# mLSTM values by direction with alternating head halves, queries split in the projections, output weights loaded over items 8 to 13

## The chip, the cores and the metric

The kernel runs on one core of a Trainium2 chip. The metric is device time in microseconds of one execution. In the rows of the profile PE is the matrix engine (TensorE), PEld its weight loads, DVE the vector engine, ACT the scalar engine, POOL GpSimd and SP the engine that issues the DMAs.

## The reference

One layer of a hybrid backbone in float32: 1024 latent tokens of width 1024, with 256 context tokens as a prefix. What the layer computes, cut to what matters:

```python
px = modulate(rms_norm(x, g_pre_mix), sh_m, sc_m) @ w_in        # pc: the same for ctx
aqx, akx, avx, mqx, mkx, mvx, mox, mgx = split(px)
att_x = window_attention(rope(aqx), rope(akx), avx, kc_att, vc_att, attn_sink)
    # 8 query heads of 64 on 2 key heads; one softmax over keys within 128,
    # all 256 context keys and a sink
h = mlstm_bidir(...)     # 4 heads, keys of 64, values of 128, forward plus backward scan:
    # num = (q k' * w_intra) v + w_inter * C q ; den = the same sums with v = 1
    # h = num / max(|den|, exp(-m))
ml_x = rms_norm(h) * g_mlstm_out * sigmoid(mox)
x = x + gt_m * rms_norm(concat(att_x, ml_x) @ w_out) * g_post_mix
x = x + gt_f * rms_norm(swiglu(modulate(rms_norm(x), ...))) * g_post_ffn
```

## The kernel before

Large products run as three passes: each operand is split into a high part in a rounded float32 format (`fp32r` in the rows) and the low rest, and `mm3` sums high*high, high*low and low*high in PSUM. `split` (L56) does it with an ACT cast (L58) and a DVE subtraction (L59). Matmuls on plain float32 operands, as in the mLSTM values, appear as two instructions each in the profile.

The stages follow each other: adaLN vectors and normalised tokens; the projections; attention with mLSTM; the output projection with the second norm; the feed-forward layer (from about 590 us to the end). The change touches the second, the third and the seam to the fourth.

**Projections** (about 140 to 306 us). Thirteen tiles of 128 output features (`TILES`: mLSTM keys and queries, attention keys and queries, output gates) are computed by `tproj` over 8 slices of the contraction, for 1024 tokens in two PSUM banks and, for three tiles, 256 context columns in a third. Four banks are in rotation. `conv` or `rope` empties them. An attention query tile (`aq0` to `aq3`) is rotated into buffer `s0` and stored to `aq_d` in DRAM by two DMAs (L619). Between tiles, `state_step` advances the mLSTM states of both directions: PE transposes keys, DVE weights them, PE multiplies with the values, DVE adds. DVE also accumulates the remaining adaLN rows (L492).

**Attention with mLSTM** (about 306 to 497 us) runs over 16 items: block n of 128 tokens times key head g. `Soft(i).scores(h)` multiplies a query head with up to 384 window keys and 256 context keys (L778, L779) and DVE masks and reduces (L780); `norm` takes exponentials on ACT (L789) and normalises on POOL (L794). `Values(i)` transposes the probabilities (`tr`, L808), splits them, and multiplies by the values (`mm`, L818, L819). Queries come from DRAM as one tile `qd` (`q_load`, L564) and are split by POOL (`q_split`, L570, L571). Scores are computed two items ahead.

Items 0 to 7 also do one block of mLSTM each: `ml_scores` of the next block (L693, eight half-height instructions that alternate the two 64-row head halves), `ml_values` four times (two directions times two head halves), `ml_norm`, and `ml_out` of the block before. One `ml_values` call takes one bank: for each of two head pairs a matmul of the query rows with the state (64 rows, L707) and one of the weights with V (128 rows, L708); then DVE forms the denominator (L711 to L713), and ACT (forward, L717) or DVE (backward, L719) scales the two heads out of the bank. `state()` tiles, mLSTM queries and weights live in the same 16 slots `R(k)` that the output weights take later.

PSUM in this stage: three banks `pt` for transposes, mLSTM values and `ml_out`, one bank `po`, and two double banks `s` for scores. `PLAN_ML` and `PLAN` give the order in which the steps of an item are written down. The order on each engine is made from it by a planner that plays the program through with costs of its own and lets ready instructions pass. From item 14 on, and in all later stages, the order is written by hand (`manual_schedule`): there items 14 and 15 are interleaved with the output projection of block 0, `omm(0, 1, ..)` for the mLSTM half and, at the end, `omm(0, 0, ..)` for the attention half, into `ops_[0]`.

The eight output weight tiles (`wout_load`) are read in the order 7 to 0 in items 9 to 13: DMA, an ACT cast (L749) and a POOL subtraction (L750); the last one goes in two halves through the buffers of `qd`, with ACT and DVE (L58, L59).

Of the kernel before, what the change touches and what calls it, by code (L numbers as in the profile page):

```python
# [16 lines left out]
P = 128  # L17
# [16 lines left out]
PLAN_ML = "T0 q A0 A1 A2 A3 T1 T2 T3 M0 M1 T4 V0 N0 M2 V1 M3 M4 O z V2 w V3 s N1 x"  # L34
PLAN = "T0 q A0 A1 A2 A3 T1 T2 T3 N0 M0 T4 M1 M2 N1 M3 M4 O z l"


def body(tc, x, ctx, vecs, bcv, bada, gqm, gqf, wada, ws1, ws2, wt, wout, wfi, wfo,
# [377 lines left out]
    aq_d = tc.dram_tile([8, 64, S], F32, name="aq_d")  # L416
# [13 lines left out]
    def tproj(j, with_ctx):  # L430
        wh, wl = tws.pop(j)
        ps = [pa.tile([P, 512], F32, name=f"t{j}_{i}", tag="mm", bufs=4) for i in range(3 if with_ctx else 2)]
        for kt in range(KT):
# [3 lines left out]
            if with_ctx:  # L437
                mov.append((ch[b][:, k, :], cl[b][:, k, :]))
            outs = [ps[0], ps[1]] + ([ps[2][:, :L]] if with_ctx else [])
            for o, m in zip(outs, mov):  # L440
                pe.matmul(o, wh[:, kt], m[0], start=f, stop=False)  # L441
                pe.matmul(o, wh[:, kt], m[1], start=False, stop=False)  # L442
            for o, m in zip(outs, mov):
                pe.matmul(o, wl[:, kt], m[0], start=False, stop=l)  # L444
        return ps
# [111 lines left out]
    qds, qhl, prs, wo = {}, {}, {}, {}  # L557
# [8 lines left out]
    def q_split(i):  # L566
        qd = qds.pop(i)
        qh = qq.tile([P, 4, P], F32R, name="qh", tag="qh", bufs=2)
        ql = qq.tile([P, 4, P], F32R, name="ql", tag="ql", bufs=2)
        pool.tensor_scalar(qh, qd, 1.0, 1.0, MUL, MUL)  # L570
        pool.tensor_tensor(ql, qd, qh.bitcast(F32), SUB)  # L571
        qhl[i] = qh, ql
# [16 lines left out]
    for j, name in enumerate(TILES):  # L589
# [38 lines left out]
        if name == "aq3":  # L628
# [3 lines left out]
            for i in range(2):  # L632
                q_load(i)
                q_split(i)
# [65 lines left out]
    def ml_values(n, d, hb):  # L700
# [3 lines left out]
        r = slice(hb * 64, hb * 64 + 64)  # L704
        pv = bank().rearrange("p a b -> p (a b)")[:, 0:258].rearrange("p (j v) -> p j v", j=2)
        for j in range(2):
            pe.matmul(pv[:, j, :], qp_[r, d, j, :], cs[r, j, :], start=True, stop=False)  # L707
            pe.matmul(pv[:, j, :], wt_[:, d, 2 * j + hb, :], V[:, n, 2 * j + hb, :], start=False, stop=True)  # L708
        dn = qa.tile([P, 2], F32, name="dn", tag="dn", bufs=8)
        den = pv[:, :, 128]  # L710
        dve.tensor_tensor(dn, den, emcol[:, r0 + hb:r0 + 4:2], MAX)  # L711
        dve.scalar_tensor_tensor(dn, den, -1.0, dn, MUL, MAX)
        dve.reciprocal(dn, dn)  # L713
        for j in range(2):
            t = hs[:, 2 * j + hb]
            if d == 0:
                act.activation(t, pv[:, j, 0:128], AF.Copy, scale=dn[:, j:j + 1])  # L717
            else:
                dve.scalar_tensor_tensor(t, pv[:, j, 0:128], dn[:, j:j + 1], t, MUL, ADD)  # L719
# [18 lines left out]
    def wout_load(j):  # L738
        h, l = R(2 * j, f"woh{j}", (D,), F32R), R(2 * j + 1, f"wol{j}", (D,), F32R)
        if j == 0:  # L740
            for i in range(2):
                sl = slice(i * 512, (i + 1) * 512)
                load_split(h[:, sl], l[:, sl], wout[j][:, sl],
                           qq.tile([P, 4, P], F32, name="wor0", tag="qd", bufs=2).rearrange("p a b -> p (a b)"))
            wo[j] = h, l
            return
        raw = R(2 * j - 1, f"wor{j}", (D,))
# [83 lines left out]
    for i in range(2):  # L831
# [5 lines left out]
        if i == 0:  # L837
            q_load(2)
            ml_scores(0)

    for i in range(NIT):
# [6 lines left out]
        for k in (PLAN_ML if i < NT else PLAN).split():  # L848
# [862 lines left out]
```

## Time and profile before

| | us |
|---|---|
| median of 3 runs (lowest, highest) | 1239.06 (1238.37, 1239.9) |
| the profiled execution, its own time | 1238.05 |
| its span | 1236.3 |
| projections of 13 tiles | about 140 to 306 |
| items 0 to 7 (with mLSTM) | about 310 to 437 |
| items 8 to 13 | about 437 to 482 |
| items 14 and 15, block 0 of the output projection | about 482 to 502 |

The granted clock of PE is full in all these stretches. Rows of grouped instructions give line, engine, operation, output and inputs, shapes, count, then busy microseconds, mean nanoseconds of one, and the idle time of the engine ahead of them with what ended it. Rows of a timeline give start and length in microseconds; a bracket holds the idle time before and its releaser. Rows of waits give the total, the count and the longest. Matmuls are pipelined: the distance between starts tells more than a row's length.

### The profile page before, as it was taken

To read this page: it belongs to the slowest core of one execution; us is meant where nothing else is said; L and a number is where in the kernel's file an instruction comes from. 1 tells how busy PE (TensorE), PEld (TensorE's weight loads), DVE (VectorE), ACT (ScalarE), POOL (GpSimd) and SP (SyncE) were. 2 spreads that over 40 slices of the span, in tenths; PEclk is the share of its full clock that TensorE was granted. 3 is DMA by queue.
4 is the path that set the end of the run, shared out by engine and by line. 5 is a ranking of instruction groups with operands and counts; after the bars stand their busy time and mean duration, and the time that the engine had idled before them with its cause. 6 is when DMAs were issued, how large, how long until landed. Compare 5 with 4: busy or idle time off the path is not lost.

```text
span 1236.3 us, 16232 instructions
## 1 busy us (share of the span) xinstructions
PE 1193.3 (97%) x5859; PEld 971.0 (79%) x5859; DVE 798.9 (65%) x1375; ACT 579.9 (47%) x1111; POOL 205.1 (17%) x245
## 2 busy tenths in 40 slices
PE   7889999999999998999899999999999999999996
PEld 1789878877777786888678888888888888888885
DVE  3882277862877787355767677767777746554566
ACT  4654533111666796677633333333333325434542
POOL 0752401244644475000000000000000000000000
PEclk9899999999999999999999999999999999999999
DMA  9432855656433320522024465675644647665853
GB/s 339 157 114 73 302 161 153 190 144 194 130 86 86 113 76 10 204 80 74 17 90 137 174 226 191 214 245 190 220 154 161 202 155 257 206 216 191 306 170 119
DMA packets 90953, 201.78 MB, mean 163 GB/s; under 512 B 9077, under 2 KB 29941, under 8 KB 89465
## 3 DMA queue, kind: packets, MB, share of 16 engines
q1 hardware_dynamic: 90872, 200.74, 48.8%
q8 instruction: 46, 0.75, 0.3%
q14 instruction: 35, 0.28, 0.1%
HBM read 149.32 MB, written 50.73 MB: 162 GB/s over the span
## 4 chain that ended last, share of the span: by engine, by line
PE 65%; DVE 4%; ACT 3%; POOL 1%; DMA 1%; issue 1%; DVEq 0%; ACTq 0%
PE xv L72 7%; PE xv L71 7%; PE xv L70 7%; PE pt L72 5%; PE pt L71 5%; PE pt L70 5%; PE pt L708 2%; PE pt L707 2%; PE pt L808 2%; PE fx L70 1%; PE op L72 1%; PE op L70 1%; PE op L71 1%; PE fx L72 1%; PE fx L71 1%; PE s L778 1%
## 5 line engine op out<-in xcount | busy, mean ns | idle before, releaser
L59 DVE TENSOR_TENSOR fo<-fr,fo 128x1024 fp32r<-128x1024 f32 x77 | 92.7, 1222 | 71.2 <-ACT fo L58 60.8
L58 ACT CAST fo<-fr 128x1024 fp32r<-128x1024 f32 x77 | 79.7, 1051 | 73.9 <-PE pt L72 36.5
L441 PE MATMUL t<-hh,th 128*128 128x512 f32 x208 | 82.6, 397 | 1.7 <-ACT cr L458 1.7
L442 PE MATMUL t<-hl,th 128*128 128x512 f32 x208 | 82.2, 395 | 0.0
L58 ACT CAST wS<-wr 128x512 fp32r<-128x512 f32 x88 | 54.1, 622 | 56.3 <-PE pt L72 37.4
L59 DVE TENSOR_TENSOR wS<-wr,wS 128x512 fp32r<-128x512 f32 x88 | 60.4, 689 | 19.9 <-ACT wS L58 19.9
L70 PE MATMUL xv<-tT,wS 128*128 128x512 f32 x168 | 66.9, 398 | 4.9 <-ACT tT L1083 2.3
L444 PE MATMUL t<-hh,tl 128*128 128x512 f32 x208 | 68.3, 393 | 0.0
L72 PE MATMUL xv<-tT,wS 128*128 128x512 f32 x168 | 66.2, 394 | 0.3 <-DVE wS L59 0.3
L71 PE MATMUL xv<-tT,wS 128*128 128x512 f32 x168 | 66.3, 395 | 0.0
L492 DVE SCALAR_TENSOR_TENSOR acc<-wb,csil,acc 128x1024 f32<-128x1024 f32 x24 | 34.4, 1432 | 40.1 <-DMA wb<-in_wada 40.0
L441 PEld LDWEIGHTS t<-hh,th 128*128 128x128 f32 x208 | 39.1, 188 | 10.4 <-ACT cr L458 2.1
L944 DVE TENSOR_TENSOR wr<-wr 128x512 f32<-128x512 f32 x66 | 45.5, 690 | 1.5
L1195 ACT ACTIVATE es<-es 128x512 f32<-128x512 f32 x22 | 13.9, 632 | 67.8 <-DVE es L947 67.8
L442 PEld LDWEIGHTS t<-hl,th 128*128 128x128 f32 x208 | 39.1, 188 | 8.1 <-issue 1.2
L444 PEld LDWEIGHTS t<-hh,tl 128*128 128x128 f32 x208 | 38.3, 188 | 7.9 <-issue 1.0
L70 PE MATMUL op<-woh,mh 128*128 128x512 f32 x112 | 44.3, 395 | 0.0
L72 PE MATMUL op<-woh,ml 128*128 128x512 f32 x112 | 43.8, 391 | 0.0
L71 PE MATMUL op<-wol,mh 128*128 128x512 f32 x112 | 43.7, 390 | 0.0
L72 PE MATMUL pt<-fo 128*128 128x512 f32 x110 | 42.8, 389 | 0.0
L71 PE MATMUL pt<-fo 128*128 128x512 f32 x110 | 42.8, 389 | 0.0
L70 PE MATMUL pt<-fo 128*128 128x512 f32 x110 | 42.8, 389 | 0.0
(982 smaller groups left out, 3491.0 us busy)
## 6 DMA issues: line engine op xcount, KB each, us to landing
wr<-in_wfi SPq DMA_DIRECT2D x44, 512.0 KB, 4.7
wb<-in_wada SPq DMA_DIRECT2D x24, 512.0 KB, 4.3
s_d<-a SPq DMA_DIRECT2D x22, 512.0 KB, 6.6
bt<-in_wfo SPq DMA_DIRECT2D x44, 256.0 KB, 3.6
tb_d<-bt SPq DMA_DIRECT2D x11, 1024.0 KB, 3.9
fr<-s_d SPq DMA_DIRECT2D x44, 256.0 KB, 4.2
fr<-tb_d SPq DMA_DIRECT2D x44, 256.0 KB, 4.5
fr<-a_d SPq DMA_DIRECT2D x33, 256.0 KB, 4.5
```

Source lines behind the costliest of these rows:

```text
L58: act.copy(hi, raw)
L59: dve.tensor_tensor(lo, raw, hi.bitcast(F32), SUB)
L70: pe.matmul(ps, a[0], b[0], start=first, stop=False, **kw)
L71: pe.matmul(ps, a[0], b[1], start=False, stop=False, **kw)
L72: pe.matmul(ps, a[1], b[0], start=False, stop=last, **kw)
L441: pe.matmul(o, wh[:, kt], m[0], start=f, stop=False)
L442: pe.matmul(o, wh[:, kt], m[1], start=False, stop=False)
L444: pe.matmul(o, wl[:, kt], m[0], start=False, stop=l)
L492: dve.scalar_tensor_tensor(a, t, csil[:, kt, 0:1], a, MUL, ADD)
L707: pe.matmul(pv[:, j, :], qp_[r, d, j, :], cs[r, j, :], start=True, stop=False)
L708: pe.matmul(pv[:, j, :], wt_[:, d, 2 * j + hb, :], V[:, n, 2 * j + hb, :], start=False, stop=True)
L944: dve.tensor_tensor(out, a, b, SUB)
```

## The change

`ml_values` takes a whole direction and two banks. It first does the four 64-row matmuls, alternating the head halves and with them the two banks, then the four 128-row ones; the reciprocal is taken once a direction. The four steps V0 to V3 of an item become V0 and V1.

The attention queries are split where they are projected (ACT and DVE); high and low part go to two DRAM tensors, and `q_load` fetches both. The step `q` is gone.

`tproj` does the context columns after the token columns.

The output weights are read in the order 0 to 7 in items 8 to 13, all with ACT and POOL, the raw tile in the slot of the next tile's high part. With them, the four attention-half steps of block 0's output projection (P0 to P3) move from the end of the hand-written part into item 13 (`PLAN13`).

```diff
-PLAN_ML = "T0 q A0 A1 A2 A3 T1 T2 T3 M0 M1 T4 V0 N0 M2 V1 M3 M4 O z V2 w V3 s N1 x"
-PLAN = "T0 q A0 A1 A2 A3 T1 T2 T3 N0 M0 T4 M1 M2 N1 M3 M4 O z l"
+PLAN_ML = "T0 A0 A1 A2 A3 T1 T2 T3 M0 M1 T4 V0 N0 M2 M3 M4 O z V1 w s N1 x"
+PLAN = "T0 A0 A1 A2 A3 T1 T2 T3 N0 M0 T4 M1 M2 N1 M3 M4 O z l"
+PLAN13 = "T0 A0 A1 A2 A3 m T1 T2 P0 T3 N0 M0 T4 M1 P1 M2 N1 M3 P2 M4 O P3 l"
+WLOADS = {8: (0, 1), 9: (2,), 10: (3,), 11: (4,), 12: (5, 6), 13: (7,)}
...
-    aq_d = tc.dram_tile([8, 64, S], F32, name="aq_d")
+    aq_d = [tc.dram_tile([8, 64, S], F32, name=f"aq_d{p}") for p in "hl"]
...
-            if with_ctx:
-                mov.append((ch[b][:, k, :], cl[b][:, k, :]))
...
+        for kt in range(KT if with_ctx else 0):
+            b, k = kt // 4, kt % 4
+            mm3(ps[2][:, :L], (wh[:, kt], wl[:, kt]), (ch[b][:, k, :], cl[b][:, k, :]), kt == 0, kt == KT - 1)
...
-        qd = qds[i] = qq.tile([P, 4, P], F32, name="qd", tag="qd", bufs=2)
-        for d in range(2):
-            dma(qd[64 * d:64 * d + 64], aq_d[4 * g:4 * g + 4, :, n * P:(n + 1) * P].rearrange("h d t -> d h t"))
...
-        pool.tensor_scalar(qh, qd, 1.0, 1.0, MUL, MUL)
-        pool.tensor_tensor(ql, qd, qh.bitcast(F32), SUB)
+        qhl[i] = [qq.tile([P, 4, P], F32R, name=f"q{p}", tag=f"q{p}", bufs=3) for p in "hl"]
+        for t, src in zip(qhl[i], aq_d):
+            for d in range(2):
+                dma(t[64 * d:64 * d + 64].bitcast(F32), src[4 * g:4 * g + 4, :, n * P:(n + 1) * P].rearrange("h d t -> d h t"))
...
             rope(ps, t, 0.125)
-            for g in range(2):
-                dma(aq_d[4 * g + i], t[64 * g:64 * g + 64])
+            qp2 = R(3, f"aqh{i}", (S,), F32R), t.bitcast(F32R)
+            split(*qp2, t)
+            for d, o in zip(aq_d, qp2):
+                for g in range(2):
+                    dma(d[4 * g + i], o[64 * g:64 * g + 64].bitcast(F32))
...
-    def ml_values(n, d, hb):
+    def ml_values(n, d):
...
-        pv = bank().rearrange("p a b -> p (a b)")[:, 0:258].rearrange("p (j v) -> p j v", j=2)
+        pv = [bank().rearrange("p a b -> p (a b)")[:, 0:258].rearrange("p (j v) -> p j v", j=2) for hb in range(2)]
         for j in range(2):
-            pe.matmul(pv[:, j, :], qp_[r, d, j, :], cs[r, j, :], start=True, stop=False)
-            pe.matmul(pv[:, j, :], wt_[:, d, 2 * j + hb, :], V[:, n, 2 * j + hb, :], start=False, stop=True)
...
+            for hb in range(2):
+                r = slice(hb * 64, hb * 64 + 64)
+                pe.matmul(pv[hb][:, j, :], qp_[r, d, j, :], cs[r, j, :], start=j == 0, stop=False,
+                          skip_group_check=j > 0)
+        for hb in range(2):
+            for j in range(2):
+                pe.matmul(pv[hb][:, j, :], wt_[:, d, 2 * j + hb, :], V[:, n, 2 * j + hb, :], start=False, stop=True,
+                          skip_group_check=j > 0)
...
-        raw = R(2 * j - 1, f"wor{j}", (D,))
+        raw = R(2 * j + 2, f"wor{j}", (D,)) if j < 7 else V.rearrange("p n h v -> p (n h v)")[:, 0:D]
...
-                for j in {9: (7,), 10: (6,), 11: (5, 4), 12: (3, 2), 13: (1, 0)}[i]:
+                for j in WLOADS[i]:
                     wout_load(j)
+            elif op == "m":
+                msplit(0, 0)
+                ops_[0] = pb.tile([P, 1024], F32, name="op", tag="s", bufs=2)
+            elif op == "P":
+                omm(0, 0, range(n, n + 1))
...
-    msplit(0, 0)
     b2.tr(3)
     omm(0, 1, range(3, 4))
     mm_t(b2, 2, 3)
     b2.out()
-    omm(0, 0, range(4))
```

More of the change, by code (lines that the diff above doesn't have):

```diff
@@ L703, in ml_values @@
         cs = state(d, s_)
-        r = slice(hb * 64, hb * 64 + 64)
-        pv = bank().rearrange("p a b -> p (a b)")[:, 0:258].rearrange("p (j v) -> p j v", j=2)
+        pv = [bank().rearrange("p a b -> p (a b)")[:, 0:258].rearrange("p (j v) -> p j v", j=2) for hb in range(2)]
         for j in range(2):
[L707 to L719, printed above, removed]
+            for hb in range(2):
[6 more added lines that the diff above has]
+                          skip_group_check=j > 0)
+        dn = qa.tile([P, 2, 2], F32, name="dn", tag="dn", bufs=4)
+        for hb in range(2):
+            den = pv[hb][:, :, 128]
+            dve.tensor_tensor(dn[:, hb], den, emcol[:, r0 + hb:r0 + 4:2], MAX)
+            dve.scalar_tensor_tensor(dn[:, hb], den, -1.0, dn[:, hb], MUL, MAX)
+        dve.reciprocal(dn, dn)
+        for hb in range(2):
+            for j in range(2):
+                t = hs[:, 2 * j + hb]
+                if d == 0:
+                    act.activation(t, pv[hb][:, j, 0:128], AF.Copy, scale=dn[:, hb, j:j + 1])
+                else:
+                    dve.scalar_tensor_tensor(t, pv[hb][:, j, 0:128], dn[:, hb, j:j + 1], t, MUL, ADD)
     def ml_norm(n):
@@ L839, in body, with msplit, omm @@
             ml_scores(0)
+    ops_, mhl = {}, {}
+    def msplit(n, hf):
+        h, l = (qq.tile([P, 4, P], F32R, name=f"m{x_}{hf}", tag=f"q{x_}", bufs=3) for x_ in "hl")
+        split(h, l, mix[n][:, 4 * hf:4 * hf + 4, :])
+        mhl[n, hf] = h, l
+    def omm(n, hf, ks):
+        h, l = mhl[n, hf]
+        first, last = (0, 7) if n == 0 else (4, 3)
+        for k in ks:
+            j = 4 * hf + k
+            for i in range(2):
+                sl = slice(i * 512, (i + 1) * 512)
+                mm3(ops_[n][:, sl], (h[:, k], l[:, k]), (wo[j][0][:, sl], wo[j][1][:, sl]), j == first, j == last)
     for i in range(NIT):
@@ L847, in body @@
             break
-        for k in (PLAN_ML if i < NT else PLAN).split():
+        for k in (PLAN_ML if i < NT else PLAN13 if i == NIT - 3 else PLAN).split():
             op, n = k[0], int(k[1:] or 0)
-            if op == "q" and a:
-                q_split(i + 2)
-            elif op == "w" and i + 1 < NT:
+            if op == "w" and i + 1 < NT:
                 ml_load(i + 1)
@@ L871, in body @@
                 ml_out(i - 1)
-            elif op == "l" and i > NT:
-                for j in {9: (7,), 10: (6,), 11: (5, 4), 12: (3, 2), 13: (1, 0)}[i]:
+            elif op == "l":
+                for j in WLOADS[i]:
                     wout_load(j)
+            elif op == "m":
[3 more added lines that the diff above has]
+                omm(0, 0, range(n, n + 1))
     order = tc.manual_schedule()
     order.__enter__()
-    ops_ = {0: pb.tile([P, 1024], F32, name="s", tag="s", bufs=2)}
-    mhl = {}
-    def msplit(n, hf):
-        h, l = (qq.tile([P, 4, P], F32R, name=f"m{x_}{hf}", tag=f"q{x_}", bufs=2) for x_ in "hl")
-        split(h, l, mix[n][:, 4 * hf:4 * hf + 4, :])
-        mhl[n, hf] = h, l
-    def omm(n, hf, ks):
-        h, l = mhl[n, hf]
-        for k in ks:
-            j = 4 * hf + k
-            for i in range(2):
-                sl = slice(i * 512, (i + 1) * 512)
-                mm3(ops_[n][:, sl], (h[:, k], l[:, k]), (wo[j][0][:, sl], wo[j][1][:, sl]), j == 4, j == 3)
     def mm_t(b, *ts):
```

22 lines of the change are left out of this document (4 added, 18 removed).

## The prediction

> **What bounds the kernel now.** I read the page first (shares, chain of waits), then busy time by engine over stretches of the attention stage, then the order of instructions on TensorE in one item.
>
> ```profile
> span 1236.3 us, 16232 instructions
> PE 1193.3 (97%) x5859; PEld 971.0 (79%) x5859; DVE 798.9 (65%) x1375; ACT 579.9 (47%) x1111; POOL 205.1 (17%) x245
> ...
> PE 65%; DVE 4%; ACT 3%; POOL 1%; DMA 1%; issue 1%; DVEq 0%; ACTq 0%
> ```
>
> The profiled execution took 1238.05 us, 1.75 more than its span. TensorE (PE) is busy nearly everywhere and most of the chain that can be followed is PE. So an edit is worth what it takes off PE, or off a wait of PE. The edits lie in the projections and in the attention stage. For these, busy time by stretch (length; then busy us and count of PE, PEld, DVE, ACT, POOL; clock; DMA share):
>
> ```profile
> 360.10:375.40 15.30, 15.24 (x93) 11.90 (x92) 11.63 (x37) 9.64 (x28) 6.14 (x9) 1.00 0.31 86
> 310.10:436.90 126.80, 124.59 (x744) 98.51 (x745) 97.19 (x312) 86.35 (x239) 62.77 (x82) 1.00 0.38 109
> 436.90:470.40 33.50, 32.21 (x212) 27.55 (x212) 31.38 (x71) 29.65 (x67) 28.60 (x29) 1.00 0.14 40
> 470.40:484.40 14.00, 10.15 (x61) 7.61 (x59) 11.73 (x25) 10.75 (x27) 9.84 (x11) 1.00 0.01 3
> 484.40:501.80 17.40, 17.33 (x85) 14.10 (x86) 8.71 (x14) 6.89 (x12) 0.00 (x0) 1.00 0.23 68
> ```
>
> One of the eight items with mLSTM work lasts 15.3 us, with PE at 15.24 and DVE at 11.63: PE sets its length, and DVE is the next engine. In the items after them (436.9 on) PE, DVE and ACT are all near full. From 470.4 to 484.4 PE idles 3.85 us. After that PE is full again.
>
> **The mLSTM values.** This is PE's work at the end of an item (start, length, line):
>
> ```profile
> 372.04 0.49 PE L707 MATMUL pt<-cs,qp 64*128 64x129 f32 x2
> 372.45 0.49 PE L708 MATMUL pt<-V,wl 128*128 128x129 f32 x2
> ...
> 374.96 0.49 PE L708 MATMUL pt<-V,wl 128*128 128x129 f32 x2
> 375.38 0.72 PE L693 MATMUL s<-mq,mk 64*128 64x128 f32 x8
> 376.02 0.44 PE L778 MATMUL s<-k,qh 128*128 128x384 f32 x1
> ```
>
> Each matmul of the program is two instructions here (x2). Eight such pairs, half-height (64 rows, L707) and full-height (128 rows, L708) by turns, go from 372.04 to 375.38: 3.34 us a direction, 0.417 a pair. Right behind, the scores L693 are eight half-height instructions of the same size, whose code alternates the two head halves: from 375.38 to 376.02, 0.64 in all. The weight loads show what is lost in the first kind, and a run of one height what a step costs:
>
> ```profile
> 357.19 0.19 PEld L708 LDWEIGHTS pt<-V,wl 128*128 128x128 f32 x1
> 357.30 0.19 PEld L708 LDWEIGHTS pt<-V,wl 128*128 128x128 f32 x1
> 357.61 0.18 PEld L707 LDWEIGHTS pt<-cs,qp 64*128 64x128 f32 x1
> 465.48 0.28 PE L778 MATMUL s<-k,qh 128*128 128x256 f32 x1
> 465.60 0.28 PE L779 MATMUL s<-k,ql 128*128 128x256 f32 x1
> ```
>
> Inside a pair the second load follows after 0.11; to a load of the other height it takes 0.31. Full-height instructions of one kind in a row step by 0.12.
>
> The change does four half-height matmuls with the halves by turns, then four full-height ones. I cost the first eight instructions like L693, 0.64 (129 columns for 128). The second eight are seven steps of 0.118 and a last one of 0.31 to the next kind, 1.13. Together 1.77 for 3.34: 1.57 less a direction, **3.14 an item**. PE's 15.24 becomes 12.1. No run of eight full-height instructions of this type is in the trace, so the 1.13 is bounded: 0.94 (eight times 0.118) and 1.67 (four times 0.417). I take 1.13, as the 0.11 inside a pair is the same instruction.
>
> DVE is next. The rows of three items (count, busy, mean, idle before), and the evacuation behind one values step:
>
> ```profile
> L711 DVE TENSOR_TENSOR dn<-pt,emcol 128x2 f32<-128x2 f32 x12 | 1.9, 158 | 8.8 <-PE pt L708 8.7
> L713 DVE RECIPROCAL dn<-dn 128x2 f32<-128x2 f32 x12 | 1.5, 154 | 0.0
> 360.23 0.16 DVE L711 TENSOR_TENSOR dn<-pt,emcol 128x2 f32<-128x2 f32 x1 [1.36 <-PE pt L708]
> 360.77 1.13 DVE L719 SCALAR_TENSOR_TENSOR hs<-pt,dn,hs 128x128 f32<-128x128 f32 x4
> 366.71 0.88 DVE L780 CUSTOM_DVE_ANT_0 pr__3495<-s,mask,bcr 128x640 f32<-128x640 f32 x1
> ```
>
> Two reciprocals of 0.15 fewer an item leave DVE at 11.3, below PE's 12.1. The two banks of a direction are already emptied together (four L719 in one row), from 360.23 to 361.90: 1.67. Holding both banks costs nothing new while PE has 1.67 of work that needs no bank: scores of the next item (L693, L778). If that cover is gone, the 1.67 lies on PE. Between PE's 12.1 and DVE's 11.3 with its waits (8.7 us in three items, 2.9 each, so 14.2) I take 12.4, near PE, since PE's idle time is under 0.1 an item today. So 15.3 to 12.4, eight times: **-23.2**. Ends: -25.1 (3.14 times eight, PE alone) and -8.8 (1.1 times eight, DVE with all its waits).
>
> **The query split.** Two POOL instructions an item go, and four times one ACT cast and one DVE subtraction of 128x1024 come into the projections, with twice the stores and twice the loads by SP.
>
> ```profile
> 309.91 0.62 POOL L570 TENSOR_SCALAR qh<-qd 128x512 fp32r<-128x512 f32 x1 [6.53 <-PE s L778]
> 310.61 1.28 POOL L571 TENSOR_TENSOR ql<-qd,qh 128x512 fp32r<-128x512 f32 x1
> 312.62 0.55 PE L808 MATMUL pt<-cst,pr__2713 128*128 128x128 f32 x3 [1.03 <-POOL pr__2713 L794]
> ```
>
> POOL has 6.14 of 15.3 busy in an item, so 1.9 less there is hidden. Only at the stage's start does it stand ahead of the normalising that PE waits for: the 1.03 goes, **-1.0** (ends 0 and -1.9).
>
> ```profile
> 205.00:270.00 65.00, 65.00 (x350) 50.81 (x349) 53.31 (x76) 11.56 (x16) 14.49 (x8) 1.00 0.58 174
> 252.77 1.05 ACT L58 CAST th<-tw 128x1024 fp32r<-128x1024 f32 x1 [10.61 <-PE t L442]
> 255.72 1.21 DVE L59 TENSOR_TENSOR tl<-tw,th 128x1024 fp32r<-128x1024 f32 x1
> 257.82 1.29 DVE L475 SCALAR_TENSOR_TENSOR aq<-t,cost 128x512 f32<-128x512 f32 x2 [0.89 <-DMA aq_d<-aq]
> PE t L441 <- ACT cr L458: 1.7, 1, 1.7
> ```
>
> The added cast and subtraction cost as these same shapes, 1.05 and 1.21 a tile. DVE goes from 53.3 to 58.2 of 65 and PE stays full: **0**. The cover is thin in one place. The rope of the next tile already waits 0.89 for the store of the last one out of the same buffer, and the low part now leaves 2.3 later. Queued behind that DVE instruction are the state steps and weight splits that PE waits for. Exposed three times, +6.9. The extra SP issues and loads fall in stretches with a DMA share of 0.31 to 0.58. The context columns, done last, might take away PE's one wait of 1.7 for a bank; but the copy that frees it also waits for the convolution's own buffer, so I take 0. Ends of this part: -1.7 and +6.9.
>
> **Output weights and the first half-projection.**
>
> ```profile
> 482.04 0.50 PE L819 MATMUL po<-tl__4825,av 128*128 128x512 f32 x1 [1.15 <-DVE tl__4825 L59]
> 496.34 0.39 PE L70 MATMUL s<-woh,mh 128*128 128x512 f32 x1
> 501.78 0.39 PE L70 MATMUL op<-woh,mh 128*128 128x512 f32 x1
> 496.54 0.58 ACT L826 COPY o<-po 64x512 f32<-64x512 f32 x1 [1.73 <-PE po L819]
> 497.14 1.14 ACT L58 CAST mh<-mix 128x512 fp32r<-128x512 f32 x2
> L749 ACT CAST woh<-wor x7: 1041/1046/1047, 412.0 to 449.1; 128x1024 fp32r<-128x1024 f32 x7
> ```
>
> The 24 matmuls from 496.34 to 501.78 (5.44 us) move into item 13, where PE idles 3.85 between waits like the 1.15 for DVE; I let them fill 3.0. But today these 24 hide the evacuation of the last item and the split of the next rows. Without them PE has nothing from about 496.4 until the copy and the first cast are done, about 497.8, and the low part is late too: +1.6. Most of the weight casts (from 412.0) run today under items that PE binds; all eight now come after them, where ACT has 40.4 of 47.5 busy, and some five more (5.2) would nearly fill it: +1.0. Net **-0.4** (ends -2.5, if all idle time is filled and the gap is 1.4, and +5, if nothing is filled and 3 of the casts' time shows).
>
> **Sum**: -23.2 - 1.0 + 0 - 0.4 = -24.6, from the profiled 1238.05 to 1213.5. The median of the runs is 1.0 above that execution, so 1214.5, rounded **1215**; its own range is 1209 to 1221.
>
> **Rivals.**
> 1. One of the two runs does not overlap. Either the halves in two banks step by 0.118 (1.13 instead of 0.64 a direction), or full-height instructions in a row keep the 0.417 a pair (1.67 instead of 1.13). Either is about 1.0 an item, +8: **1223**. For: no such run is in the trace. Against: L693 and the 0.11. A rule of the Trainium skill, TensorE: Matmul & The Clock Gate, Part 3 (Packing small matmuls), says that a weight load overlaps a running matmul only at another row group, which is the second form. The 0.11 between two loads of 0.19 at full height does not agree; by the rule the time would be 1223, by the row 1215.
> 2. DVE binds the items. It keeps its 2.9 of waits for L708 and the item lasts 14.2: -8.8 - 1.4, **1229**. For: the 8.7. Against: the step waited for is itself halved. The Trainium skill has the rule behind it, TensorEngine Tiling (Array Packing), PSUM Bottleneck: tiling speeds TensorE, not the evacuation. The trace neither shows nor excludes it yet.
> 3. The banks. Two of three bank tiles are taken at once; the next transposes or values wait until both are emptied, behind a score reduction of 0.88: 2.55 a direction, 5.1 an item, 2.0 more than is gained, eight times, less 1.4: **1253**, slower. It decides when the exposed wait passes 1.57 a direction. Against: from 310 to 436 PE waits 0.5 in all for a bank that DVE empties behind the values, and the scores lie between.
>
> ```profile
> PE pt L808 <- DVE hs L719: 0.5, 1, 0.5
> ```
>
> 4. The planner undoes it by putting attention matmuls of the other kind between the new ones, as it does between today's pairs; then only 1 to 2 us are gained: **1238**.
>
> **How the numbers follow.** Chances: the forecast 0.62, rivals 0.15, 0.14, 0.04, 0.05 in order. Faster is the forecast with rivals 1 and 2, 0.91; the same (within 0.2%, 2.5 us, about what this kernel's runs can tell) is the fourth, 0.05; slower the third, 0.04. Rivals 3 and 4 are left out of the range; its upper end takes in the second. All low ends together (-25.1, -1.9, -1.7 and -2.5) make -31.2, which is 1208 beside the median; I allow 2 more for step lengths read to a hundredth: **1206 to 1230**.
>
> **What would show it.** Right: L693-like steps for the half-height values, about 1.8 us a direction, items of 12 to 12.7 with PE full, a gap of 1 to 2 us on PE ahead of the second row's projection. Wrong: PE waits for DVE L719 or ACT L717 by the microsecond (rivals 2, 3), half-height pairs still 0.4 apart (1, 4), waits of DVE for the query stores that show on PE in the projections, or weight casts ahead of attention splits on ACT after the eighth item.

## The result

The changed kernel took 1232.84 us (median of 7 runs, 1229.89 to 1235.68) against 1239.06 (median of 7, 1237.77 to 1240.13): 0.9949 of the time before, with a 95% interval of 0.9934 to 0.9964. The forecast was 1215. It is faster, by 6.2 us where 24 were forecast. The profiled execution took 1232.62, its span 1230.8.

The page of the changed kernel, the lines that answer to those shown of before:

```profile
span 1230.8 us, 16261 instructions
PE 1184.8 (96%) x5859; PEld 965.4 (78%) x5859; DVE 801.0 (65%) x1361; ACT 583.2 (47%) x1114; POOL 177.5 (14%) x214
...
PE 62%; DVE 6%; ACT 5%; issue 1%; DMA 1%; POOL 0%; DVEq 0%; SPq 0%; ACTq 0%
```

PE's busy time fell by 8.5 us and the span by 5.5. DVE and ACT now hold 11% of the chain together where they held 7%.

To see where, I cut the attention stage at three events of PE's queue: the first transpose of probabilities (the start-up of the stage ends), the last mLSTM values matmul, and the first transpose of the next stage. Busy time by these two stretches (length; then busy us and count of PE, PEld, DVE, ACT, POOL; clock; DMA share and GB/s), first of before, then of after:

```profile
312.62:436.87 124.25, 123.14 (x732) 97.42 (x733) 94.73 (x304) 84.80 (x235) 60.30 (x79) 1.00 0.38 110
436.87:510.50 73.63, 68.05 (x391) 55.88 (x390) 54.66 (x112) 52.68 (x112) 38.47 (x39) 1.00 0.21 71
```

```profile
317.33:430.10 112.77, 109.93 (x730) 91.42 (x729) 94.84 (x289) 79.66 (x229) 40.11 (x57) 1.00 0.50 142
430.10:506.70 76.60, 69.59 (x395) 56.18 (x393) 54.15 (x112) 56.83 (x117) 37.06 (x36) 1.00 0.20 69
```

The mLSTM stretch is 11.5 shorter where 23.2 were forecast, the stretch behind it 3.0 longer where 0.4 less was forecast, and the first transpose comes 4.7 later (317.33 for 312.62). Together 3.8 us earlier at the next stage (506.7 for 510.5). ACT's column shows one of the moves: 5.1 us of its work left the first stretch and 4.2 came into the second.

**One values step.** The order on PE, in the timeline of after:

```profile
372.81 0.71 PE L705 MATMUL pt<-cs,qp 64*128 64x129 f32 x4
373.45 0.71 PE L709 MATMUL pt<-V,wl 128*128 128x129 f32 x4
374.09 0.72 PE L690 MATMUL s<-mq,mk 64*128 64x128 f32 x8
374.64 0.61 PE L705 MATMUL pt<-cs,qp 64*128 64x129 f32 x4
375.18 0.71 PE L709 MATMUL pt<-V,wl 128*128 128x129 f32 x4
375.65 0.42 PE L775 MATMUL s<-k,qh 128*128 128x384 f32 x1
```

This isn't the order in which the code is written. The planner took the matmuls bank by bank: four half-height instructions of one head half (L705), the four full-height ones that finish that bank (L709), and then the same for the other half. The halves never alternate, and each direction changes height three times inside. The steps are 0.64, 0.64, 0.54 and 0.47. Full height runs at 0.12 an instruction (four in 0.47, with other work behind them). One item, from one direction's first full-height matmul to the same of the next item, as a stretch with the columns above:

```profile
368.11:381.77 13.66, 13.42 (x91) 11.12 (x91) 11.68 (x36) 9.50 (x28) 4.33 (x7) 1.00 0.43 118
```

So it is 13.66 long, with PE nearly full, where 12.4 was forecast.

**The start of the stage.** SP's queue, then the other engines, in the timeline of after:

```profile
269.53 2.18 SPq L617 DMA_DIRECT2D aq_dh<-aqh  x2
273.44 1.36 SPq L567 DMA_DIRECT2D qh<-aq_dh  x2
...
279.22 2.60 SPq L575 DMA_DIRECT2D qb<-w_d  x4
...
306.17 3.38 POOL L578 TENSOR_TENSOR qb<-qb,mq 128x128 f32<-128x128 f32 x8 [3.02 <-DMA qb<-w_d]
312.31 0.19 POOL L764 COPY pr__2732<-bcr 128x4 f32<-128x4 f32 x1 [2.76 <-issue]
312.52 0.75 DVE L777 CUSTOM_DVE_ANT_0 pr__2732<-s,mask,bcr 128x512 f32<-128x512 f32 x1 [1.94 <-POOL pr__2732 L764]
313.33 0.39 PE L775 MATMUL s<-k,qh 128*128 128x256 f32 x1 [2.26 <-DVE sm L777]
314.00 0.58 PE L775 MATMUL s<-k,qh 128*128 128x256 f32 x1
```

The broadcasts for the mLSTM queries (`qb`) stand behind the stores and the eight loads of the first queries, and issue at 279.2 (270.0 before). POOL's products with them, and the store of the last product, end later; POOL's copy into the first probability tile comes 2.76 after that (the row says "issue"; in a run below the same copy is released by a store of these products); DVE's first score reduction waits for the copy; PE waits 2.26 us for DVE. Then something that I had not expected: matmuls of 0.28 us take 0.58 and 0.41. The stretch from 314 on, in the columns above, shows the granted clock at 0.50:

```profile
314.00:317.00 3.00, 3.00 (x16) 2.55 (x16) 2.16 (x7) 2.52 (x8) 0.79 (x2) 0.50 0.95 312
```

### The profile page after: what moved, and what is told of

Its sections match the earlier page's. It is cut to its first block, busy times and chain, and to the rows that moved or that the text cites. A ratio compares the mean times of both kernels' runs of the same rounds, so it can differ in the third digit from the quotient of the medians.

```text
span 1230.8 us, 16261 instructions
## 1 busy us (share of the span) xinstructions
PE 1184.8 (96%) x5859; PEld 965.4 (78%) x5859; DVE 801.0 (65%) x1361; ACT 583.2 (47%) x1114; POOL 177.5 (14%) x214
## 4 chain that ended last, share of the span: by engine, by line
PE 62%; DVE 6%; ACT 5%; issue 1%; DMA 1%; POOL 0%; DVEq 0%; SPq 0%; ACTq 0%
PE xv L74 7%; PE xv L72 7%; PE xv L73 7%; PE pt L74 5%; PE pt L72 5%; PE pt L73 5%; PE op L74 2%; PE op L73 2%; PE op L72 2%; PE fx L72 1%; PE fx L74 1%; PE fx L73 1%; PE pt L709 1%; PE pt L705 1%; PE fy L72 1%
## 5 line engine op out<-in xcount | busy, mean ns | idle before, releaser
L443 PE MATMUL t<-hh,tl 128*128 128x512 f32 x208 | 65.3, 392 | 0.0
L72 PE MATMUL op<-woh,mh 128*128 128x512 f32 x128 | 51.0, 398 | 1.8 <-ACT mh L60 1.8
L74 PE MATMUL op<-woh,ml 128*128 128x512 f32 x128 | 50.2, 392 | 0.1
L73 PE MATMUL op<-wol,mh 128*128 128x512 f32 x128 | 49.9, 390 | 0.0
L775 PE MATMUL s<-k,qh 128*128 128x256 f32 (+1 forms) x128 | 41.8, 335 | 3.9 <-DVE sm L777 2.9
L73 PE MATMUL pt<-fo 128*128 128x512 f32 x110 | 42.8, 389 | 0.0
L74 PE MATMUL pt<-fo 128*128 128x512 f32 x110 | 42.8, 389 | 0.0
```

Source lines behind the costliest of these rows:

```text
L72: pe.matmul(ps, a[0], b[0], start=first, stop=False, **kw)
L73: pe.matmul(ps, a[0], b[1], start=False, stop=False, **kw)
L74: pe.matmul(ps, a[1], b[0], start=False, stop=last, **kw)
L775: pe.matmul(o, qh[:, h, :], k2[g][:, kc], start=True, stop=False)
```

## The experiments

Thirteen kernels, each timed in five rounds beside the kernel before. Beside the time, I give the two stretches cut as above: "mLSTM" from the first transpose to the last values matmul, "behind" from there to the first transpose of the next stage. Before they are 124.2 and 73.6, after 112.8 and 76.6.

### The order of the values held

```diff
+        with tc.manual_schedule(engines={mybir.EngineType.PE}):
             for j in range(2):
                 for hb in range(2):
                     ... the four half-height matmuls
             for hb in range(2):
                 for j in range(2):
                     ... the four full-height matmuls
```

> The changed kernel, with the order of the eight TensorE matmuls of one direction held as the source writes it (head halves by turns, then the four full-height ones). Theory A (the planner's regrouping by bank took the missing half of the gain): the eight half-height instructions take about 0.64 us, as L693 does, the steady item goes from 13.66 to 12.2 to 12.8 us, and the time falls by 7 to 12 us against the changed kernel, to 1221 to 1226. Rival B (VectorE or the two banks set the item, not the order): the item stays within 0.2 us of 13.66, the idle time moves to PE behind DVE L723, and the time stays within 2 us of 1232.8.

1226.51 us, 0.9902 of before (0.9882 to 0.9923), where the changed kernel has 0.9949 (0.9934 to 0.9964). Its timeline of one direction, and one whole item as a stretch:

```profile
377.63 0.71 PE L706 MATMUL pt<-cs,qp 64*128 64x129 f32 x6
378.27 1.16 PE L710 MATMUL pt<-V,wl 128*128 128x129 f32 x8
379.18 0.48 PE L817 MATMUL po<-tl__3588,av 128*128 128x512 f32 x1
```

```profile
364.98:378.27 13.29, 12.86 (x92) 10.38 (x91) 11.65 (x36) 9.58 (x29) 4.33 (x6) 1.00 0.48 121
```

The eight full-height instructions take 0.91 (378.27 to 379.18). Of the eight half-height ones six stand together here, in 0.64; in the other direction they run among the eight of the mLSTM scores, sixteen in 1.19 (368.38 to 369.57). Added up from one start to the next over an item, the values and these scores take 4.1 us, where after has 5.1 and before 7.0. So the item lost 2.9 where the forecast had 3.14. But it lasts 13.17 (the one shown 13.29, the next 13.04) and not 12.4: PE idles 0.2 to 0.4 an item where it idled 0.06, and the steps of the attention matmuls grew by the rest. The mLSTM stretch is 107.5. Theory A holds, though the time is 6.3 us under the changed kernel for the 7 to 12 expected, and the item above the 12.2 to 12.8. DVE is busy 11.5 of 13.2: it isn't full.

### The loads of the queries behind the broadcasts

```diff
-            for i in range(2):
-                q_load(i)
             ...
                 ml_queries(k // 2, k % 2)
+            if name == "aq3":
+                for i_ in range(2):
+                    q_load(i_)
```

> The changed kernel, with the loads of the first two items' queries issued behind the broadcasts of the mLSTM queries (only the order on SP's queue differs). Theory C (the eight loads and the four late stores ahead of the broadcasts delay the mLSTM queries, and POOL's copy for the first attention block stands behind them): the broadcasts issue about 6 us earlier, the last POOL product of a broadcast ends near 303 instead of 309.55, PE's wait of 2.26 us at 313 and the half clock after it go, and the time falls by 2.5 to 4.5 us, to 1228 to 1230. Rival D (the chain is as long as its transfers and POOL's products, whatever the order): PE's wait at 313 stays above 1.5 us, and the time stays within 1 us of 1232.8. If only the wait goes and the clock stays at half, the fall is 2.3.

1231.57 us, 0.9937 (0.9919 to 0.9955). In its timeline SP issues the broadcasts first, and POOL's copy comes 5.8 us earlier:

```profile
272.90 2.97 SPq L575 DMA_DIRECT2D qb<-w_d  x4
...
306.48 0.19 POOL L765 COPY pr__2732<-bcr 128x4 f32<-128x4 f32 x1 [3.00 <-DMA q_dr<-qb]
...
314.48 1.00 PE L806 MATMUL pt<-cst,pr__2732 128*128 128x128 f32 x4
```

PE's wait and the half clock are gone. From the first scores to the first transpose it takes 4.8 us (309.6 to 314.5), where before took 5.8 (306.85 to 312.62) and after 7.5 (309.85 to 317.33). So the query split does save the 1.0 that was forecast for the start, and the queue order cost 2.6 there, half clock included (it lies ahead of the first transpose). The time fell by 1.3 only, for the 2.5 to 4.5 expected, and the intervals overlap. The next stage's first transpose comes 2.3 earlier than in after (504.4 for 506.7), but this execution had half clock at two places where after had none, 149 to 152 in the projections and 596 to 599 in the feed-forward layer. Theory C is shown in the trace, not settled in the time.

### The values alone

The kernel before with `ml_values` from after; queries and output weights as before:

```diff
-PLAN_ML = "T0 q A0 A1 A2 A3 T1 T2 T3 M0 M1 T4 V0 N0 M2 V1 M3 M4 O z V2 w V3 s N1 x"
+PLAN_ML = "T0 q A0 A1 A2 A3 T1 T2 T3 M0 M1 T4 V0 N0 M2 M3 M4 O z V1 w s N1 x"
...
-                ml_values(i, n // 2, n % 2)
+                ml_values(i, n)
```

> The kernel before, with the mLSTM values by direction alone (queries and output weights as before). Theories A and C and E (the new order gives 1.6 us an item as the planner places it; the query split costs 3 to 4 at the stage's start; the weight casts cost about 4 in the items after the mLSTM): this kernel has the gain without the two losses, 10 to 13 us against the kernel before, 1226 to 1229, faster than the changed kernel by 4 to 7. Rival (the values themselves are worth only what the changed kernel shows, and the rest of the change is free): 1231 to 1234.

1237.45 us, 0.9987 (0.9975 to 0.9999). Neither theory had that. The stretches, with the one at half clock below them (0.51 of full speed over 6.9 us):

```profile
314.90:431.10 116.20, 112.26 (x732) 92.78 (x733) 93.88 (x286) 84.70 (x233) 60.27 (x79) 1.00 0.40 110
431.10:512.00 80.90, 71.67 (x391) 57.80 (x389) 56.70 (x114) 52.74 (x113) 38.44 (x39) 0.96 0.20 68
477.80:484.70 6.90, 5.43 (x17) 4.46 (x18) 4.08 (x7) 1.76 (x3) 0.00 (x0) 0.51 0.00 0
```

The timeline of the place where it was lost:

```profile
474.75 2.73 POOL L801 TENSOR_SCALAR pr__4728<-pr__4728,sm 128x512 f32<-128x512 f32 x4
475.23 3.38 DVE L59 TENSOR_TENSOR wol<-wor,woh 128x512 fp32r<-128x512 f32 x2
478.54 0.67 DVE L834 TENSOR_TENSOR mix<-po,o 64x512 f32<-64x512 f32 x1
479.26 0.80 PE L825 MATMUL po<-th__4737,av 128*128 128x512 f32 x1 [3.24 <-DVE mix L834]
```

The mLSTM stretch gained 8.0, and the stretch behind lost 7.3 of it. Two subtractions of the last output weight (L59) stand ahead of the addition that empties `po` (L834). PE waits 3.24 for it, and then works at half clock from there to 484.7, 5.4 us of which half are lost. In the kernel before, DVE does this addition ahead of the two subtractions (477.8 and 479.0), and PE waits 0.7 for it. I first took POOL's total for the cause ("theory G": POOL is full from 450 to 475), which the next runs test.

### The weights and the half-projection undone

```diff
-WLOADS = {8: (0, 1), 9: (2,), 10: (3,), 11: (4,), 12: (5, 6), 13: (7,)}
+WLOADS = {8: (), 9: (7,), 10: (6,), 11: (5, 4), 12: (3, 2), 13: (1, 0)}
...
-        for k in (PLAN_ML if i < NT else PLAN13 if i == NIT - 3 else PLAN).split():
+        for k in (PLAN_ML if i < NT else PLAN).split():
...
+    msplit(0, 0)
     b2.tr(3)
     omm(0, 1, range(3, 4))
     mm_t(b2, 2, 3)
     b2.out()
+    omm(0, 0, range(4))
```

> The changed kernel, with the loads of the output weights and the first half-projection put back where they were (weights 7 to 0 from item 9 on, the 24 matmuls behind the last item). Theory E (all eight casts of 1.05 us stand in items that ScalarE binds): the casts start near 410 again, PE's waits of 1.15 and 1.48 us behind splits in the items after the mLSTM go or shrink, and the time falls by 1 to 4 us, to 1229 to 1232. Rival F (the casts cost nothing, and the moved matmuls fill idle time): the time rises by 1 to 3 us, to 1234 to 1236.

1234.8 us, 0.996 (0.9941 to 0.998): not told apart from the changed kernel. The stretch behind is 73.4, 3.2 less, but the mLSTM stretch is 117.4, 4.6 more. So the sum is 1.5 longer. The two mLSTM items from about 402 on lose most of it: there the first weight casts wait on ACT for their loads (2.1 us at 410), and PE waits 1.2 for an attention split behind such a cast. The last weight is still split whole by ACT and POOL here, as in the changed kernel. Neither E nor F is decided by this run.

### The values undone, the queries undone

The changed kernel with the values of before:

```diff
-                ml_values(i, n)
+                ml_values(i, n // 2, n % 2)
```

> The changed kernel with the mLSTM values as they were before, pair by pair (query split and output weights stay changed): the values' worth inside the changed kernel, where taken alone on the kernel before they were worth only 2. Theory G (the same 1.6 us an item is lost later unless POOL and ScalarE are relieved there, and in the changed kernel they are): the item is 15.2 to 15.4 us again, the last values come about 12 us later, and the time is 7 to 12 us above the changed kernel, 1240 to 1245. Rival (the items behind the mLSTM are bound by ScalarE and VectorE whatever PE does, so the 1.6 an item is worth 2 here too): 1233 to 1236.

1243.8 us, 1.0044 (1.0031 to 1.0057): slower than before. The stretches are 123.8 and 76.3, so the values are worth 11.0 in the mLSTM stretch here and next to nothing behind it, and the rest of the change, by itself, costs about 5. Theory G's numbers fit, though not only G's.

And the changed kernel with one array of queries again, split on POOL in every item:

```diff
-            split(*qp2, t)
-            for d, o in zip(aq_d, qp2):
-                for g in range(2):
-                    dma(d[4 * g + i], o[64 * g:64 * g + 64].bitcast(F32))
+            for g in range(2):
+                dma(aq_d[4 * g + i], t[64 * g:64 * g + 64])
...
+                q_split(i)
...
+            if op == "q" and a:
+                q_split(i + 2)
```

> The changed kernel with the queries split on POOL in every item again, from one array in DRAM (values and output weights stay changed). Theory G: POOL, which has 29.6 us busy of the 33 from 437 to 470 in the changed kernel, gets 1.9 us an item more there and is full to the last item; the last scores start 3 to 6 us later, while PE's waits of 2.26 us and the half clock at the stage's start go (minus 3.5 to 4); the time is 1232 to 1238. If POOL's share is nothing, as the prediction had it: 1228 to 1230.

1239.99 us, 1.0007 (0.9995 to 1.0019). The stretches are 115.5 and 80.5, each with one stretch of half clock (331 to 335, 461 to 465). POOL is busy 29.9 of the 30 from 437 to 467, and PE waits 3.7 for ACT at the next stage's first transpose, where after has 1.1. The time is 7 above the changed kernel, and above what either theory expected.

### Both orders; and three weights early

First the two orders together; then also other rows of the working buffers for the weights, so that three of eight loads come in items 6 and 7:

```diff
-WLOADS = {8: (0, 1), 9: (2,), 10: (3,), 11: (4,), 12: (5, 6), 13: (7,)}
+WLOADS = {6: (0,), 7: (1, 2), 8: (3,), 9: (4,), 10: (5,), 11: (6,), 12: (7,)}
+WROWS = ((1, 2), (4, 5), (6, 7), (0, 3), (9, 11), (10, 12), (13, 15), (14, 8))
...
```

> The changed kernel with the order of the eight value matmuls held (minus 6.3 alone) and the queries' first loads behind the broadcasts (minus 1.3 alone). If the two add up: 1225. If the stage's start had only hidden behind something else: 1226.5.

1226.8 us, 0.9902 (0.9887 to 0.9917): the same as the order of the values alone, while the profiled span is 1.9 shorter (1222.8 for 1224.7). The 1.3 us of the queries' order is too small for these runs' times. In the trace the start of the stage, from the first scores to the first transpose, is 2.2 shorter (4.8 for 7.0); 1.7 went again in the feed-forward layer, where this execution had half clock at 588 to 592 and that of the order alone had none at that place.

> The same with both orders, and with the output weights in other rows of the working buffers, so that three of the eight loads, casts and subtractions come in items 6 and 7, which PE binds. Theory E (casts of 1.05 us on ScalarE and subtractions of 2.4 us on POOL hold up the items behind the mLSTM): 2 to 4 us under the kernel with both orders, 1221 to 1223, and PE's waits of 1.5 and 1.2 us behind splits shrink. Rival F (they fit in without cost, VectorE alone binds these items): within 1 us of the kernel with both orders.

1224.22 us, 0.9879 (0.9862 to 0.9895). The stretches of both kernels, first without and then with the early weights:

```profile
312.67:419.90 107.23, 104.95 (x729) 85.99 (x729) 94.25 (x289) 80.32 (x229) 40.16 (x56) 1.00 0.58 157
419.90:496.80 76.90, 69.61 (x395) 56.18 (x394) 54.35 (x114) 56.54 (x117) 37.62 (x36) 1.00 0.20 70
```

```profile
315.79:423.00 107.21, 104.21 (x723) 85.01 (x724) 93.87 (x287) 83.82 (x232) 47.77 (x60) 1.00 0.57 151
423.00:496.60 73.60, 68.83 (x399) 56.82 (x398) 53.85 (x116) 53.19 (x114) 29.88 (x33) 1.00 0.27 85
```

Of the work, 3.5 us of ACT and 7.6 of POOL moved forward, under PE, at no cost there (107.2 in both); behind, 3.3 us went. In the time that is 2.6, with overlapping intervals.

### What the splitting of the weights costs, and the half-projection alone

```diff
-        dma(raw, wout[j])
-        act.copy(h, raw)
-        pool.tensor_tensor(l, raw, h.bitcast(F32), SUB)
+        for t in (h, l):
+            dma(t.bitcast(F32), aq_d[0][0:2].rearrange("h d t -> (h d) t"))
```

> The kernel with both orders, without the splitting of the output weights: both parts of each weight row block come from the queries' array in DRAM, already rounded, so the eight casts, the eight subtractions on POOL and the output weights themselves are left out (the projection multiplies other numbers, in as many matmuls). It sizes what the splitting costs behind the mLSTM. Theory E: the stretch from the last mLSTM values to the last attention scores, 40.7 us with both orders and 37.6 with three loads early, falls to 34 to 36, and the time to 1219 to 1222. Rival F (VectorE binds these items, ScalarE and POOL are only full beside it): 39 to 41 us and 1225 to 1227.

The kernel leaves out the output weights themselves: 1221.04 us, 0.9847 (0.9824 to 0.987). The mLSTM stretch is 107.2 again, and the one behind:

```profile
420.50:493.50 73.00, 68.17 (x396) 56.10 (x394) 53.21 (x114) 50.24 (x109) 18.88 (x28) 1.00 0.30 105
```

All eight casts and subtractions cost 3.9 behind the mLSTM (76.9 to 73.0), 5.8 in the time. Moving three of them forward gives back 3.3 of the 3.9. From the last values to the last scores it is 36.6, where both orders have 40.8 (34 to 36 were expected of theory E, 39 to 41 of F). That is 0.6 over E's range, and the time is inside it. So E holds, and F, by which they cost nothing, falls. With POOL at 18.9 of 73 the stretch is only 0.6 shorter than with POOL at 29.9 (73.0 for 73.6): what is left is hardly POOL's.

On the kernel with both orders and early weights:

```diff
-        for k in (PLAN_ML if i < NT else PLAN13 if i == NIT - 3 else PLAN).split():
+        for k in (PLAN_ML if i < NT else PLAN).split():
...
     b2.out()
+    omm(0, 0, range(4))
```

> The kernel with both orders and three weight loads early, with the first half-projection (24 matmuls) put back behind the last item, as it was before the change. By the prediction's sum the move is worth 1.4 (3.0 of filled idle time less a gap of 1.6), without its casts: the time rises by 1 to 2 us, to 1225 to 1226, PE's wait of 1.3 us for the cast of the next rows goes and idle time of 3 to 4 us comes between 455 and 475. If the move is worth nothing: 1224 within 0.7.

1222.05 us, 0.9861 (0.9839 to 0.9882). It was expected to rise; it fell by 2.2, and the stretch behind by as much:

```profile
421.90:493.30 71.40, 68.74 (x399) 57.05 (x398) 53.84 (x116) 53.04 (x114) 29.56 (x33) 1.00 0.28 89
```

The intervals overlap, so the time alone doesn't settle it; the trace says that the move of the half-projection costs here. The waits name the place (total, times, longest; with the move, then without it):

```profile
PE op L73 <- ACT mh L61: 1.8, 2, 1.3
PE op L73 <- ACT mh L61: 0.5, 1, 0.5
```

PE's wait for the cast of the next rows is 1.3 longer with the move, and its wait for ACT at the next stage's first transpose 0.8 longer (1.2 for 0.4): together the 2.2.

### The order held on the kernel before

The kernel with the values alone, and the `manual_schedule` line of the first experiment around its eight matmuls.

> The kernel before, with the values by direction and the order of their matmuls held (queries and weights as before). Theory G (POOL, full from 450 to 475 in the kernel with the values alone, takes the gain of the mLSTM items back): the items last 13.1 to 13.4 us, the last values come 5 to 6 us earlier than with the values alone, and the time is within 2.5 us of that kernel's 1237.4. Rival (the gain of the order adds as it did on the changed kernel): 1231.

1227.87 us, 0.9904 (0.9883 to 0.9925). Theory G said 1235 to 1240, and falls. The stretches:

```profile
314.40:423.80 109.40, 104.20 (x724) 85.17 (x725) 92.76 (x282) 82.92 (x229) 58.42 (x76) 1.00 0.40 116
423.80:499.50 75.70, 69.61 (x399) 56.98 (x397) 56.03 (x118) 55.08 (x118) 40.48 (x42) 1.00 0.24 79
```

POOL does the same work as with the values alone (98.7 us there, 98.9 here) and is as full (25.0 of the 25 from 442 to 467), and nothing is taken back: the stretch behind is 5.2 shorter. What the values alone lost there was thus no matter of POOL's total. The two subtractions of the last weight are here too, but DVE does the addition ahead of them (466.8 and 468.0), PE waits 0.7 for it, and the clock stays full.

### The late chain taken away

The kernel with the values alone, its last weight split as the other seven: one cast on ACT, one subtraction on POOL, no subtractions on DVE:

```diff
-        if j == 0:
-            ... two halves with load_split
-            return
-        raw = R(2 * j - 1, f"wor{j}", (D,))
+        raw = R(2 * j - 1, f"wor{j}", (D,)) if j else V.rearrange("p n h v -> p (n h v)")[:, 0:D]
```

> The kernel before with the values by direction, and the last weight row block split as the other seven (one cast on ScalarE, one subtraction on POOL) in place of two halves on ScalarE and VectorE. Theory H (one late chain: the two VectorE subtractions, 0.68 us and 2.78 us beside a busy POOL, stand ahead of an addition that PE waits 3.24 us for, and the clock is half for 3.4 us after that): the wait falls under 2, the half clock there goes, and the time falls from 1237.4 to 1231 to 1234. Theory G (POOL's total, now 2.4 us more): 1237 to 1240.

1231.01 us, 0.9928 (0.9912 to 0.9943), 6.4 under the values alone, although POOL has more to do (41.0 us behind the mLSTM for 38.4). The stretch behind:

```profile
429.30:504.30 75.00, 68.56 (x392) 56.04 (x390) 53.26 (x112) 52.64 (x112) 40.98 (x40) 1.00 0.19 66
```

PE's longest wait in the stage behind (total, times, longest):

```profile
PE po L818 <- DVE mix L827: 1.7, 1, 1.7
```

The wait fell from 3.2 to 1.7, the clock stays full, and the stretch is 5.9 shorter. Theory H is shown: one late chain and the half clock with it ate most of the gain of the values. The half clock lasted longer than that theory had it, 6.9 us and not 3.4.

### The queries on POOL in the fastest kernel

The kernel with the half-projection behind the last item, with the queries split on POOL as in the diff further up.

> The fastest kernel so far (held order, three weight loads early, half-projection behind the last item, 1222.1) with the queries split on POOL again, item by item. If the query split relieves POOL where it binds (theory G): POOL full from 437 to 465, and 1226 to 1230. If it is worth only POOL's 0.9 us at the start of the stage: 1222 to 1224.

1228.81 us, 0.9907 (0.9892 to 0.9922), 6.8 slower, the time that theory G gave. But G has POOL full from 437 to 465, and POOL is busy 21.2 of these 28. The timeline shows that a good part isn't POOL's load:

```profile
330.39 0.62 POOL L573 TENSOR_SCALAR qh<-qd 128x512 fp32r<-128x512 f32 x1 [8.10 <-DMA qd<-aq_d]
332.33 1.36 POOL L798 TENSOR_SCALAR pr__2762<-pr__2762,sm 128x512 f32<-128x512 f32 x2
333.07 0.33 PE L812 MATMUL pt<-cst,pr__2762 128*128 128x128 f32 x1 [3.10 <-POOL pr__2762 L798]
```

POOL sits 8.1 us in front of a query load that is late, with the normalising that PE needs behind it: 3.1 of wait, and up to 1.7 lost to the half clock from 334.0 to 337.5. The mLSTM stretch is 111.8, 4.3 longer, and these two make that up. The stretch behind is 75.0, 3.6 longer, with no wait of PE over 0.7 and the clock full; what makes these 3.6, and what of them is POOL's load, stays open.

## Why the prediction was wrong

**That PE bounds the mLSTM items** held. The stretch got shorter when PE's work did, and DVE, at 11.5 to 11.7 of 13 to 13.7 an item, was never full. Rival 2, with 14.2 an item, didn't come about, and neither did rival 3: PE waits 0.6 for a bank behind ACT L721 and 1.4 behind DVE L723 in the whole stage, no 2.55 a direction.

**The values, -23.2; measured -11.5.** The step that failed is "The change does four half-height matmuls with the halves by turns, then four full-height ones." That is the order of the code, and I costed it as the order on PE. The stage is planned, and the planner finished one bank before the other. Rival 4 had the planner, at 0.05 and with the wrong deed (foreign matmuls put between); what it did was regroup, which leaves half of the gain. Rival 1 had nearly the item (1.0 longer than forecast, where 1.26 was measured), for a reason that the trace refutes.

The prices of the runs were right: half-height by turns as L693 (sixteen in 1.19), full height 0.91 for eight where I had 1.13 with 0.94 as the low end. So the bound of 0.417 a pair, and the rule of the Trainium skill behind rival 1 (TensorE: Matmul & The Clock Gate, Part 3, Packing small matmuls), under which weight loads of one row group shouldn't overlap running matmuls, is not what this chip shows for full-height instructions in a row: 0.114 each.

With the order held the mLSTM stretch is 107.2 to 107.5, 16.8 below before. The remaining 6.4 of the 23.2 is the term "So 15.3 to 12.4": an item is 13.17, because its other work grew by 0.8, part of it idle time. Why that work takes longer there stays open.

**The query split: 0 in the projections, -1.0 at the start.** The projections came out as forecast. The first weight-by-token product to the first scores took 266.3 before and 268.6 after, but over all kernels here with the query path of before it is 266.3 to 270.3 (six, mean 268.3), and with the new one 265.7 to 269.6 (nine, mean 268.2): no difference. The -1.0 is there once the queue is in order. The sentence that failed is "The extra SP issues and loads fall in stretches with a DMA share of 0.31 to 0.58." It asked whether the DMA engines have room, and not what stands behind these issues on SP: the broadcasts. Before, POOL's copies behind them ended at 303.4 and the first scores started at 306.9, 3.5 to spare; after, the copies come behind the first scores. That cost 2.6 at the start of the stage, by the wait of 2.26 and the half clock after it. Neither a range nor a rival had it. The stores' own wait on DVE, which had the +6.9, didn't show.

**Output weights and half-projection, -0.4; measured +3.0.** Mis-sized: the casts, +1.0. Splitting the weights costs 3.9 in that stretch, subtractions on POOL included, and nearly all of it can be hidden under PE in items 6 and 7. The direction was right, and which rows of the working buffers each load has to wait for was there to be read. The moved half-projection was given -3.0 + 1.6; the gap was there (1.3 for the first cast of the next rows), and the filling wasn't: the 24 matmuls ran as one block from 472.6 to 477.7 behind the last scores, and PE's waits of 1.2 and 1.5 for DVE ahead of it stayed. Taken back, they gave 2.2, by the trace.

**The sum.** Forecast and measured at the next stage's first transpose: values -11.5, start 1.7 longer, stretch behind 3.0 longer, and 3.0 by which the first scores came late, which over the kernels is scatter and no part of the change: -3.8. The last 1.7 of the span's 5.5 came later, where the two kernels' code is the same, and it is the clock's: behind one and the same wait in the feed-forward layer half clock followed before and not after (the last section has the rows). The range was also lopsided. Its lower end added the low ends of all parts, and its upper end took rival 2 alone, without the +6.9 of the stores and the +5 of the casts that the parts themselves allowed.

The fastest kernel here that does all of the layer's work holds the order of the values, puts the first query loads behind the broadcasts, takes three weights early and leaves the half-projection where it was: 0.9861 of before, 17 us.

## What to carry to other kernels

Where a planner orders the work, a sequence of matmuls in the code is a wish: cost the order that it will make (here it finished one bank before it took up the other), or hold it. When a step adds DMAs, look for what stands behind them on the issuing queue and how much slack that has; the share of the DMA engines doesn't say. A gain in a stage that one engine binds can be lost to a single late instruction behind it: a part that is worth little when timed on its own, as the values were, may have lost its gain further on. Cut both traces at the same events and see in which stretch it went.

## What was not expected of the hardware

**Half clock after a pause.** PE's granted clock stood at 0.50 for about 3.4 us at a time, which costs up to 1.7 us of work, during or soon after a pause of PE. At the start of this stage the four kernels whose PE waited there 2.0 us or more (after, e_order, w_undo, v_undo) all show it, and the five others with the new query path, whose wait was gone, show none. But the length of the pause alone doesn't decide. In the feed-forward layer PE waits 2.24 to 2.29 us for ACT at the same place in all fifteen kernels, and half clock follows within 1.5 us in nine of them, before among these, and not in the other six, after among these. The 4 us from PE's return, before and after:

```profile
602.00:606.00 4.00, 4.00 (x11) 2.97 (x12) 2.62 (x5) 3.56 (x6) 0.00 (x0) 0.63 0.00 0
598.20:602.20 4.00, 4.00 (x17) 3.13 (x18) 3.29 (x6) 3.59 (x7) 0.00 (x0) 1.00 0.00 0
```

From the next stage's first transpose to the end, the nine take 725.5 to 726.0 us (q_undo, with one more such stretch, 727.3) and the six 724.1 to 724.4. A second pause there, of 1.4 to 1.6 some 6 to 8 us on, has half clock behind it in thirteen; that one doesn't show in these times. So 1.7 us between two single executions can be the clock's. In the projections a pause of 2.7 was followed by half clock (v_only) and one of 2.8 was not (v_w0); a pause of 1.5 was followed by it in q_undo, and one of 1.5 in after's last items was not. With two pauses of 1.9 and 3.2 close together (v_only) it lasted 6.9 us. The Trainium skill (TensorE: Matmul & The Clock Gate, Part 1, The HAM clock gate) states a window of about 3.4 us both ways; the length of the slow stretch agrees, while here pauses from 1.5 us on were at times enough.

**DVE beside POOL.** A subtraction of 128x512 with two inputs from SBUF took 0.68 us in one case and 2.78 in another, where POOL was normalising. The rows of the values-alone kernel, smallest, median and largest in ns:

```profile
L59 DVE TENSOR_TENSOR wol<-wor,woh x2: 677/1727/2777, 475.2 to 477.9; 128x512 fp32r<-128x512 f32 x2
```

The long one started at 475.23, POOL's four instructions in a row ended at 477.47, and it ended at 478.01. In the kernel before and in v_held the first subtraction of the same pair took 1.73 and 1.76, and there too it ended 0.54 after the last of POOL's row. One with an input from PSUM took 0.69 beside the same POOL work (v_held, at 467.41). So in these three cases the subtraction looks held until POOL's row ends, and not slowed by a factor; no run here tests that. The Trainium skill (GPSIMD Engine Reference, Specifications) says that GpSimd and VectorE share their SBUF interfaces and contend where a VectorE instruction has two SBUF inputs; this agrees.
